# One pace for attention's background steps in all three token groups of a hybrid mLSTM, attention and expert block

## Chip, cores and metric

The kernel runs on one core of a Trainium2 chip. The metric is the device time of one execution in microseconds (us). An execution has five engines that matter here, each with its own queue of instructions in a fixed order: PE (TensorE, matmuls), DVE (VectorE), ACT (ScalarE), POOL (GpSimd, which here issues the gathers) and SP (SyncE, which issues the other DMAs).

## What is computed

One decoder block on x, 1024 tokens of 1024 values, in float32:

```python
h = rmsnorm(x, norm1_g) * (1 + sc1) + sh1
mq, mk, mv, mo, mi, mf, dq, dk, dv = split(h @ w_in)
hm = rmsnorm(mlstm_chunkwise(silu(conv(mq, mk)), mv, mi, mf)) * sigmoid(mo)
od = rmsnorm(softmax(dq1 @ dk1.T) @ dv - lam * softmax(dq2 @ dk2.T) @ dv) * c
x = x + g1 * (concat(hm, od) @ w_out)
h2 = rmsnorm(x, norm2_g) * (1 + sc2) + sh2
q = h2 @ w_query
...
x = x + g2 * sum over 8 heads and 16 experts of gate * gelu(h2 . u[e]) * v[e]
out = rmsnorm(x, final_g)
```

The attention is causal, has 4 heads, and each head has two score matrices of 64 values per key (the differential form). The expert stage picks, for each token and head, 16 of 16384 experts by two half keys.

## The kernel before

The 1024 tokens are 8 blocks of 128, in three groups of 2, 3 and 3 blocks (group 0, 1, 2). Each group goes through the same front stages, one after the other: `front_T` (normalize and transpose), `front_proj` (L692, all input projections), `front_mix` (L774, what is left of attention and mLSTM, then the norm of the mixed rows, `mix_end` L644), `front_out` (projection by w_out), `front_norm2` and `front_keys` (the query projection and the top 16 of each half). After the third group comes the dense part (L1338 scores, L1370 values), in which the experts of some token blocks are computed as full matmuls over the table. For the other blocks the rows of the chosen experts are gathered: POOL issues an indirect DMA for each (gu L1024, gv L1076, gvr L1057), DVE multiplies the row of u by the token (L1028), and PE or DVE sums the rows of v (`ga` L1090 on PE, L1064 on DVE).

**Background steps.** Work that is not the main line of a group is written as Python generators. Each is an entry [generator, rate, credit] in the list `background`. `tick()` (L306) adds the rate to the credit of every entry, and takes a step of it for each whole credit:

```python
w[2] += w[1]
while w[2] >= 1.0:
    w[2] -= 1.0
    more = next(w[0], False)
```

`tick()` is called once after each 256 KB weight tile of a projection (`proj_T` L390, `proj_R` L410), after each score matmul in `att_S` (L579), and on three of four steps of the loop in `front_mix`. Other entries are the gathers (rate 1.6), the gate tables (oh L1255, ps_g L1242, stg L1244; rate 1.5) and the mLSTM steps.

**Attention's steps.** `attention(o)` (L745) works on units, one for each head and block. With nb blocks in the group it has 4 heads times nb units and 2\*4\*nb + 1 steps, that is 17 in group 0 and 25 in groups 1 and 2:

```python
att_S(units[0])
yield
for k, u in enumerate(units):
    if k + 1 < len(units):
        att_S(units[k + 1])
    yield
    att_T(u)
    att_V(u)
    yield
```

`att_S` makes the scores on PE (ps_S L605, mask L608), their maximum on DVE (ast L609), the exponentials on ACT (ae L598) and the difference on DVE (ae L618). `att_T` transposes them (ps_at L629, aT L631), `att_V` multiplies by the values (ps_o L638). The first unit of a head also loads that head's keys and values (`att_load`, akT L572, avh L574) through SP. These two tiles share one tag of two buffers, so the next head's akT can be loaded when the last score matmul of this head is done, and its avh when the last L638 is done. A third user of that tag is the row g1r (L230) that `front_out` loads.

`front_proj` first projects dq, dk and dv, then puts the entry for attention into `background` (L707, L708), and then runs the projections of the mLSTM q, k, v and output gate. Between the two lie 32 weight tiles, so 32 ticks, in every group. The rate is AR[o.k], with AR = [0.6, 0.5, 0.3] (L63). By the ticks, all 17 steps are taken in group 0 (at tick 29), 16 of 25 in group 1, and 9 of 25 in group 2. The rest is run by the loop in `front_mix`:

```python
for _ in o.att[0]:
    k += 1
    if k % 2 or k % 4 == 0:
        next(steps, None)
        tick()
```

The tile framework then places the instructions: it orders each engine's instructions by its own model of times, with the program's order as a guide. The static order of each engine is therefore the program's only roughly.

Of the kernel before, what the change touches and what calls it, by code (L numbers as in the profile page):

```python
# [28 lines left out]
HD = 4  # L29
# [22 lines left out]
def kernel(ctx: ExitStack, tc: tile.TileContext, x, c_col, ada_w, ada_b, ada_bc, n1c,  # L52
# [7 lines left out]
    LPACE = ()  # L60
    PJ = 0
    ALT = 1
    AR = [0.6, 0.5, 0.3]  # L63
    SOG = [8, 0, 8]
    DEF = 0
    N1G = 2
# [491 lines left out]
    def att_heads(t0, nb, dq, mix):  # L558

        ms = fr.tile([P, 2, NBM, HD], F32, tag="ams", name="ams", bufs=1)  # L560
        units = []
        for h in range(HD):
            for b in range(nb):
                u = Unit()
                u.h, u.b, u.i, u.end = h, b, t0 + b, t0 + nb
                u.dq, u.mix, u.ms, u.first, u.units = dq, mix, ms, b == 0, units
                units.append(u)
        return units, ms
# [52 lines left out]
    def att_T(u):  # L621

        i, e = u.i, u.e
        u.aT = []
        for s0 in range(0, i + 1, 4):
            m = min(4, i + 1 - s0)
            pt = bank("ps_at")
            for j in range(m):
                nc.tensor.transpose(pt[:, j * P:(j + 1) * P], e[:, (s0 + j) * P:(s0 + j + 1) * P], ident)  # L629
            aT = fr.tile([P, 512], F32, tag="t2", name="aT", bufs=T2)  # L630
            nc.scalar.activation(aT[:, :m * P], pt[:, :m * P], AF.Copy)  # L631
            u.aT.append(aT)

    def att_V(u):
        h, b, i = u.h, u.b, u.i
        po = bank("ps_o")
        for s0 in range(i + 1):
            nc.tensor.matmul(po[:, :P], u.aT[s0 // 4][:, s0 % 4 * P:(s0 % 4 + 1) * P], u.vh[:, s0], start=s0 == 0, stop=s0 == i)  # L638
        mv = u.mix[b][:, 512 + h * P:512 + (h + 1) * P]
        nc.scalar.activation(mv, po[:, :P], AF.Copy, scale=u.r)  # L640
        junk = fr.tile([P, P], BF16, tag="ajunk", name="ajunk", bufs=1)
        nc.scalar.activation(junk, po[:, :P], AF.Square, scale=u.r, accum_out=u.ms[:, 1, b, h:h + 1])
# [49 lines left out]
    def front_proj(o):  # L692

        n, nb, t0 = o.n, o.nb, o.t0
# [9 lines left out]
        nc.sync.dma_start(vd_d[t0 * P:t0 * P + n, :].rearrange("(b p) e -> p b e", p=P), vst[:, :nb])  # L704
        o.a_, o.b_ = mlstm_rows(o.hT, nb)
        o.mix = [fr.tile([P, D], F32, tag="rows", name="mix", bufs=RB) for _ in range(nb)]
        o.att = [attention(o), AR[o.k], 0.0]  # L707
        background.append(o.att)  # L708
        overlapped.append(o)
        o.qk = []  # L710
# [34 lines left out]
    def attention(o):  # L745

        units, o.ams = att_heads(o.t0, o.nb, o.dq, o.mix)
# [9 lines that stand above are left out]
# [694 lines left out]
    front_T(gs[0])  # L1451
    for k, o in enumerate(gs):
        front_proj(o)
        front_mix(o)
        front_out(o)
# [109 lines left out]
```

## Time and profile before

| what | us |
|---|---|
| median of 3 runs (smallest to largest) | 2989.22 (2983.14 to 2993.66) |
| the profiled execution | 2983.2 |
| its span in the trace | 2981.3 |
| PE busy in the span | 2783.4 (93%) |
| DVE busy in the span | 2382.0 (80%) |
| ACT busy, POOL busy | 973.6 (33%), 1282.8 (43%) |
| DMA, mean | 302 GB/s |

The stages by time, from the lines that run in them: group 0 to about 209.5 us, group 1's front until its mix ends at 598.5 us, its output and keys and the projections of group 2 until about 1061 us, group 2's mix until 1184 us, group 2's keys until about 1413 us, the last gate tables and gathers until 1583 us, and the dense part until the end at 2981.3 us. Busy shares over the whole span average these stages; a stage is read from its own window.

### The profile page before, as it was taken

What the parts mean: (1) busy time and instruction counts of PE and PEld (TensorE: products, weight loads), DVE (VectorE), ACT (ScalarE), POOL (GpSimd) and SP (SyncE); (2) the same over time, 40 slices, a digit from 0 to 9 for tenths busy, and PEclk for the clock granted to TensorE, in tenths of its full rate; (3) what the DMA queues carried; (4) which work ended last, traced back from release to release, by engine and by line L of the source; (5) the groups of instructions that cost most, each with busy time, mean ns of one, the idle gap of its engine ahead of it and who ended that gap; (6) DMA issues with size and microseconds to landing.
All of it is one profiled execution on the core that took longest, in us unless ns stands there. A gap on an engine that the chain in (4) does not pass through costs nothing.

```text
span 2981.3 us, 40087 instructions
## 1 busy us (share of the span) xinstructions
PE 2783.4 (93%) x13686; PEld 2076.9 (70%) x13686; DVE 2382.0 (80%) x5489; ACT 973.6 (33%) x1695; POOL 1282.8 (43%) x1083
## 2 busy tenths in 40 slices
PE   6899999689999997999995999999999999999998
PEld 5547757465556765766574878878777788877786
DVE  5634999856997687357977988889988889988876
ACT  1432344312235445232453322322322323322232
POOL 0000266654555453334654555545554444544400
PEclk9989999689999999999997999999999999999999
DMA  8745699999998888998788999999899999999962
GB/s 280 252 138 180 209 360 336 324 350 339 325 345 306 305 299 293 350 332 293 280 309 284 337 335 334 332 340 340 313 339 322 331 341 324 338 323 317 318 230 70
DMA packets 396848, 900.00 MB, mean 302 GB/s; under 512 B 34770, under 2 KB 184274, under 8 KB 392548
## 3 DMA queue, kind: packets, MB, share of 16 engines
q0 software_dynamic: 147456, 536.94, 50.1%
q1 hardware_dynamic: 249188, 360.51, 35.9%
q8 instruction: 108, 1.77, 0.2%
q14 instruction: 96, 0.79, 0.1%
HBM read 846.97 MB, written 50.35 MB: 301 GB/s over the span
## 4 chain that ended last, share of the span: by engine, by line
PE 50%; DVE 18%; DMA 13%; issue 11%; POOL 5%; ACT 2%; SPq 0%; DVEq 0%; POOLq 0%; ACTq 0%
PE ps_pj L403 11%; PE ps_dS L1338 9%; PE ps_dA L1370 9%; DMA Gt<-G_d 8%; PE ps_pj L423 7%; DVE gu L1028 4%; PE ps_g L1242 3%; PE ga L1090 3%; POOL gvr L1057 3%; DVE ga L1064 2%; DMA gu<-in_peer_u_dram,ei 2%; PE ps_S L605 2%; DVE dvs L1364 1%; DMA gv<-in_peer_v_dram,eT 1%; PE ps_tr L379 1%
## 5 line engine op out<-in xcount | busy, mean ns | idle before, releaser
L1024 POOL DMA_INDIRECT gu<-in_peer_u_dram,ei x512 | 657.3, 1284 | 928.6 <-DVE sv L912 347.9
L1370 PE MATMUL ps_dA<-dvs,W 128*128 128x512 f32 x2976 | 720.8, 396 | 56.9 <-ACT W L1348 27.4
L1338 PE MATMUL ps_dS<-dhT,us 128*128 128x512 f32 x3072 | 731.0, 391 | 1.2 <-POOL us L1331 1.2
L1370 PEld LDWEIGHTS ps_dA<-dvs,W 128*128 128x128 f32 x2976 | 566.1, 191 | 188.9 <-ACT W L1348 27.4
L1028 DVE SCALAR_TENSOR_TENSOR gu<-gu,h2r 128x1024 f32<-128x1024 f32 x512 | 620.1, 1222 | 72.3 <-DMA gu<-in_peer_u_dram,ei 59.1
L1338 PEld LDWEIGHTS ps_dS<-dhT,us 128*128 128x128 f32 x3072 | 576.2, 188 | 129.4 <-issue 8.0
L1057 POOL DMA_INDIRECT gvr<-in_peer_v_dram,ei x256 | 301.5, 1178 | 339.0 <-DVE ga L1064 184.4
L1076 POOL DMA_INDIRECT gv<-in_peer_v_dram,eT x256 | 275.8, 1077 | 266.0 <-PE ga L1090 148.2
L1064 DVE SCALAR_TENSOR_TENSOR ga<-gvr,w,ga 128x1024 f32<-128x1024 f32 x254 | 326.9, 1287 | 1.7 <-issue 0.3
L1363 ACT ACTIVATE dvs<-dv 128x512 fp32r<-128x512 f32 x248 | 155.7, 628 | 368.4 <-PE ps_dA L1370 164.5
L403 PE MATMUL ps_pj<-hT,wr 128*128 128x384 f32 (+1 forms) x768 | 233.7, 459 | 3.1 <-ACT ae L598 2.9
L403 PE MATMUL ps_pj<-h2T,wr 128*128 128x384 f32 (+1 forms) x768 | 231.2, 454 | 0.0
L1339 ACT ACTIVATE ge<-ps_dS 128x512 f32<-128x512 f32 x128 | 76.5, 598 | 424.4 <-PE ps_dS L1338 413.3
L1244 ACT ACTIVATE stg<-ps_g 128x512 f32<-128x512 f32 x128 | 134.0, 1064 | 238.0 <-PE ps_g L1242 164.1
L403 PEld LDWEIGHTS ps_pj<-hT,wr 128*128 128x128 f32 x768 | 144.9, 193 | 79.5 <-issue 9.8
L1255 DVE TENSOR_TENSOR oh<-iotah,dT 128x1024 f16<-128x1024 f16 x128 | 102.2, 804 | 118.5 <-PE ps_g L1242 94.7
L403 PEld LDWEIGHTS ps_pj<-h2T,wr 128*128 128x128 f32 x768 | 142.2, 190 | 73.3 <-issue 9.9
L423 PE MATMUL ps_pj<-wr,hT 128*128 128x256 f32 (+1 forms) x672 | 182.1, 425 | 3.5 <-DMA wr<-in_w_in_dram 2.7
L1364 DVE TENSOR_TENSOR dvs<-dv,dvs 128x512 fp32r<-128x512 f32 x248 | 171.9, 698 | 16.4 <-ACT dvs L1363 16.4
L1347 DVE SCALAR_TENSOR_TENSOR ge<-ge,Gt 128x512 f32<-128x512 f32 x128 | 87.3, 692 | 119.1 <-DMA Gt<-G_d 112.9
L423 PEld LDWEIGHTS ps_pj<-wr,hT 128*128 128x128 f32 x672 | 128.5, 197 | 45.4 <-issue 23.8
L1377 DVE TENSOR_TENSOR dacc<-dacc,ps_dA 128x512 f32<-128x512 f32 x240 | 156.1, 683 | 4.6 <-PE ps_dA L1370 4.6
(294 smaller groups left out, 3333.1 us busy)
## 6 DMA issues: line engine op xcount, KB each, us to landing
u<-in_peer_uT_dram SPq DMA_DIRECT2D x128, 512.0 KB
dv<-in_peer_v_dram SPq DMA_DIRECT2D x248, 256.0 KB
wr<-in_w_in_dram SPq DMA_DIRECT2D x168, 256.0 KB
G_d<-stg SPq DMA_DIRECT2D x32, 1024.0 KB
Gt<-G_d SPq DMA_DIRECT2D x15, 2048.0 KB
wmod<-in_ada_w_dram SPq DMA_DIRECT2D x48, 512.0 KB
wr<-in_peer_w_query_dram SPq DMA_DIRECT2D x96, 256.0 KB
wr<-in_w_out_dram SPq DMA_DIRECT2D x48, 256.0 KB
```

Of the source, the lines that this page charges most:

```text
L403: nc.tensor.matmul(out[f], w2[:, kh, f * P:(f + 1) * P], hT[:, kb, :n], start=kb == 0 and f % k == 0, stop=kb == NC - 1 and f % k == k - 1)
L423: nc.tensor.matmul(out[f], hT[:, kb, f * P:(f + 1) * P], wk[:, kh], start=kb == 0 and f % k == 0, stop=kb == NC - 1 and (f % k == k - 1 or ...
L1024: nc.gpsimd.indirect_dma_start(out=u, out_offset=None, in_=pu, in_offset=bass.IndirectOffsetOnAxis(ap=o.ei[:, k:k + 1], axis=0))
L1028: nc.vector.scalar_tensor_tensor(u, u, 1.0, o.h2, op0=OP.mult, op1=OP.mult, accum_out=o.z[:, k:k + 1])
L1057: nc.gpsimd.indirect_dma_start(out=vt, out_offset=None, in_=pv, in_offset=bass.IndirectOffsetOnAxis(ap=o.ei[:, k:k + 1], axis=0))
L1064: nc.vector.scalar_tensor_tensor(o.acc, vt, o.w[:, k:k + 1], o.acc, op0=OP.mult, op1=OP.add)
L1076: got = nc.gpsimd.indirect_dma_start(out=vt, out_offset=None, in_=pv, in_offset=bass.IndirectOffsetOnAxis(ap=o.eT[:, t:t + 1], axis=0))
L1338: nc.tensor.matmul(ps, us[:, a, c], hT[:, b, c, sl], start=c == 0 and i == 0, stop=c == NC - 1 and i == 2)
L1363: nc.scalar.activation(vs[:, 0], v, AF.Copy)
L1364: nc.vector.tensor_sub(vs[:, 1], v, vs[:, 0])
L1370: nc.tensor.matmul(pacc[tb], w[:, a, tb * P:(tb + 1) * P], vs[:, b], start=jj == 0 and i == 0, stop=jj == J - 1 and i == 2)
L1377: nc.vector.tensor_add(o, o, pacc[tb])
```

## The change

The list AR is deleted, and the rate of the attention entry is the number of its steps divided by 32: 17/32 = 0.53 in group 0, 25/32 = 0.78 in groups 1 and 2. So in every group the last step of attention is taken with the last tick of the projections, and `front_mix` is left with no step of attention, only with the mLSTM outputs and `mix_end`. The 9 and 16 steps that its loop ran in groups 1 and 2 are gone from there, and with them the 7 and 12 ticks that it gave to the other background entries. No instruction is added or removed; the order changes.

```diff
--- before.py
+++ after.py
@@ -60,7 +60,6 @@
     LPACE = ()
     PJ = 0
     ALT = 1
-    AR = [0.6, 0.5, 0.3]
     SOG = [8, 0, 8]
     DEF = 0
     N1G = 2
@@ -704,7 +703,7 @@
         nc.sync.dma_start(vd_d[t0 * P:t0 * P + n, :].rearrange("(b p) e -> p b e", p=P), vst[:, :nb])
         o.a_, o.b_ = mlstm_rows(o.hT, nb)
         o.mix = [fr.tile([P, D], F32, tag="rows", name="mix", bufs=RB) for _ in range(nb)]
-        o.att = [attention(o), AR[o.k], 0.0]
+        o.att = [attention(o), (2 * HD * nb + 1) / 32.0, 0.0]
         background.append(o.att)
         overlapped.append(o)
         o.qk = []
```

Below, rows of each engine's order stand as they are issued; x16 means 16 in a row. The line numbers of the changed kernel are one lower, since L63 is gone (L605 is L604 there).

**PE, the end of group 1.** ps_S is a score matmul, ps_at a transpose of probabilities, ps_o their product with the values, ps_tr the transposes of the mixed rows with which `front_out` begins, ga a sum of gathered rows. Before, these rows end it:

```order
L605 MATMUL ps_S<-akT,dq 128x512
L605 MATMUL ps_S<-akT,dq 128x128
L608 LDWEIGHTS identb
L608 MATMUL ps_S<-mask_gt,identb 128x128
L629 MATMUL ps_at<-ident,ae 128x128 x4
L638 MATMUL ps_o<-avh,aT 128x128 x4
L629 MATMUL ps_at<-ident,ae 128x128 x5
L638 MATMUL ps_o<-avh,aT 128x128 x5
L1044 MATMUL ga<-ident,w 128x128
L1047 MATMUL ga<-ident,ef_3993 128x128
L377 MATMUL ps_tr<-ident,mix 128x128 x24
L423 MATMUL ps_pj<-wr,mT 128x256 x10
```

Before them, back to the last `L423 ... ps_pj<-wr,hT`, stand three more units without any projection. In the changed kernel:

```order
L422 MATMUL ps_pj<-wr,hT 128x256 x8
L604 MATMUL ps_S<-akT,dq 128x128
L607 LDWEIGHTS identb
L607 MATMUL ps_S<-mask_gt,identb 128x128
L628 MATMUL ps_at<-ident,ae 128x128 x4
L1043 MATMUL ga<-ident,w 128x128
L1046 MATMUL ga<-ident,ef_3992 128x128
L637 MATMUL ps_o<-avh,aT 128x128 x4
L628 MATMUL ps_at<-ident,ae 128x128 x5
L637 MATMUL ps_o<-avh,aT 128x128 x5
L1089 MATMUL ga<-gv,strip_182 32x256 x16
L376 MATMUL ps_tr<-ident,mix 128x128 x24
```

Now the last eight matmuls of the projections stand inside the last score unit, and two units of transposes and products follow instead of five; 16 ga stand ahead of the transposes.

**PE, the switch from one head to the next in group 1.** From the last score unit (128x512 and 128x128) of a head to the first (128x384) of the next, before:

```order
L605 MATMUL ps_S<-akT,dq 128x512
L605 MATMUL ps_S<-akT,dq 128x128
L608 LDWEIGHTS identb
L608 MATMUL ps_S<-mask_gt,identb 128x128
L403 MATMUL ps_pj<-hT,wr 128x384 x16
L629 MATMUL ps_at<-ident,ae 128x128 x4
L638 MATMUL ps_o<-avh,aT 128x128 x4
L605 MATMUL ps_S<-akT,dq 128x384
L608 LDWEIGHTS identb
L608 MATMUL ps_S<-mask_gt,identb 128x128
```

and in the changed kernel:

```order
L604 MATMUL ps_S<-akT,dq 128x512
L402 MATMUL ps_pj<-hT,wr 128x384 x8
L604 MATMUL ps_S<-akT,dq 128x128
L607 LDWEIGHTS identb
L607 MATMUL ps_S<-mask_gt,identb 128x128
L628 MATMUL ps_at<-ident,ae 128x128 x4
L637 MATMUL ps_o<-avh,aT 128x128 x4
L604 MATMUL ps_S<-akT,dq 128x384
L607 LDWEIGHTS identb
L607 MATMUL ps_S<-mask_gt,identb 128x128
```

The 16 matmuls of a projection that stood between the last scores of a head and the first of the next are gone from there; this form is there twice in the changed kernel (both within the projections) and once before (in the tail).

**SP, the loads in group 1.** wr are the weight tiles, before:

```order
L574 DMA avh<-vd_d 128x5x128
L385 DMA wr<-in_w_in_dram 128x2x256 x6
L572 DMA akT<-kd_d 128x640
L385 DMA wr<-in_w_in_dram 128x2x256 x8
L574 DMA avh<-vd_d 128x5x128
L385 DMA wr<-in_w_in_dram 128x2x256 x4
L572 DMA akT<-kd_d 128x640
L385 DMA wr<-in_w_in_dram 128x2x256 x5
L385 DMA wr<-in_w_out_dram 128x2x256 x3
L574 DMA avh<-vd_d 128x5x128
```

and in the changed kernel:

```order
L573 DMA avh<-vd_d 128x5x128
L384 DMA wr<-in_w_in_dram 128x2x256 x6
L571 DMA akT<-kd_d 128x640
L384 DMA wr<-in_w_in_dram 128x2x256 x4
L573 DMA avh<-vd_d 128x5x128
L384 DMA wr<-in_w_in_dram 128x2x256 x4
L571 DMA akT<-kd_d 128x640
L384 DMA wr<-in_w_in_dram 128x2x256 x2
L573 DMA avh<-vd_d 128x5x128
L384 DMA wr<-in_w_in_dram 128x2x256 x6
L571 DMA akT<-kd_d 128x640
L384 DMA wr<-in_w_in_dram 128x2x256
```

All four loads of akT now stand among the weight tiles of w_in; the last one stood behind those of w_out before.

Two counts from the same orders: of the 512 products L1028 on DVE, 128 stand ahead of group 1's first L652 (`mix_end`) before and 134 in the change, and 256 ahead of group 2's in both; of the 1024 sums L1090 on PE (program instructions), 832 stand ahead of the dense part's first L1338 before and 800 in the change, and 1024 and 1000 ahead of its first L1370.

## Rows read from the trace of the kernel before

**Rows 1.** The page: busy time, share of the span and instructions of each engine.
```profile
PE 2783.4 (93%) x13686; PEld 2076.9 (70%) x13686; DVE 2382.0 (80%) x5489; ACT 973.6 (33%) x1695; POOL 1282.8 (43%) x1083
```

**Rows 2.** Windows: stretch us, length, busy of PE PEld DVE ACT POOL, PEclk, DMA, GB/s.
```profile
343.00:387.00 44.00, 44.00 (x169) 30.48 (x168) 41.33 (x116) 7.52 (x13) 28.58 (x25) 1.00 1.01 379
387.00:480.00 93.00, 88.50 (x319) 55.87 (x318) 90.39 (x221) 45.96 (x94) 66.12 (x46) 0.93 0.96 343
480.00:540.00 60.00, 57.19 (x308) 45.13 (x307) 50.71 (x114) 23.48 (x67) 39.58 (x34) 1.00 0.97 347
540.00:598.50 58.50, 28.15 (x83) 16.68 (x83) 51.10 (x134) 18.12 (x51) 37.19 (x30) 0.54 0.92 316
...
880.00:1061.00 181.00, 180.56 (x1085) 123.95 (x1078) 134.67 (x311) 86.14 (x166) 93.14 (x75) 0.97 0.89 308
1061.00:1159.00 98.00, 84.55 (x579) 53.13 (x577) 80.62 (x194) 48.57 (x108) 53.44 (x47) 0.95 0.89 321
1159.00:1184.00 25.00, 15.93 (x128) 12.54 (x129) 18.10 (x47) 15.24 (x30) 1.47 (x2) 0.85 0.78 268
...
1490.00:1583.00 93.00, 90.64 (x629) 69.07 (x621) 74.07 (x107) 48.48 (x53) 45.48 (x33) 1.00 0.83 296
1583.00:1610.70 27.70, 0.35 (x3) 0.26 (x3) 16.00 (x27) 2.70 (x5) 14.36 (x12) 0.50 0.94 341
1610.70:2981.00 1370.30, 1331.79 (x5760) 1089.67 (x5760) 1207.26 (x1665) 411.96 (x630) 614.37 (x494) 0.98 0.88 309
```

**Rows 3.** Waits of PE, 209.5 to 598.5 us: total us, times, longest.
```profile
PE ps_at L629 <- DVE ae L618: 16.0, 2, 10.7
PE ps_S L605 <- DMA akT<-kd_d: 7.8, 1, 7.8
PE ps_tr L377 <- DVE mix L652: 4.5, 1, 4.5
```

**Rows 4.** Timeline of PE, end of group 1: start, us, line, count, [idle before].
```profile
539.10 0.61 PE L629 MATMUL ps_at<-ident,ae 128*128 128x128 f32 x4
540.39 1.16 PE L638 MATMUL ps_o<-avh,aT 128*128 128x128 f32 x8 [0.69 <-ACT aT L631]
549.35 1.61 PE L605 MATMUL ps_S<-akT,dq 64*128 64x384 f32 x2 [7.81 <-DMA akT<-kd_d]
...
589.59 1.30 PE L629 MATMUL ps_at<-ident,ae 128*128 128x128 f32 x5 [10.71 <-DVE ae L618]
...
598.55 1.28 PE L377 MATMUL ps_tr<-ident,mix 128*128 128x128 f32 x4 [1.24 <-DVE mix L652]
```

**Rows 5.** Timeline of SP's queue: three of the loads of akT (L572).
```profile
416.48 0.34 SPq L572 DMA_DIRECT2D akT<-kd_d  x1
...
539.12 0.34 SPq L572 DMA_DIRECT2D akT<-kd_d  x1
...
1118.75 0.32 SPq L572 DMA_DIRECT2D akT<-kd_d  x1
```

**Rows 6.** Timeline of PE: the scores that need rows 5's first and third load.
```profile
434.09 0.91 PE L605 MATMUL ps_S<-akT,dq 64*128 64x384 f32 x2
...
1126.45 1.55 PE L605 MATMUL ps_S<-akT,dq 64*128 64x512 f32 x4
```

**Rows 7.** The page's costliest groups: the product of a gathered row, on DVE.
```profile
L1028 DVE SCALAR_TENSOR_TENSOR gu<-gu,h2r 128x1024 f32<-128x1024 f32 x512 | 620.1, 1222 | 72.3 <-DMA gu<-in_peer_u_dram,ei 59.1
```

**Rows 8.** Waits of PE, 1061 to 1184 us, then 1413 to 1700 us.
```profile
PE ps_g L1242 <- ACT stg L1244: 12.1, 10, 3.3
...
PE ps_dA L1370 <- ACT W L1348: 27.4, 1, 27.4
```

**Rows 9.** Timeline of SP's queue at the start of the dense part.
```profile
1582.18 0.33 SPq L1247 DMA_DIRECT2D G_d<-stg  x1
...
1591.69 22.90 SPq L1285 DMA_DIRECT2D Gt<-G_d  x2
```

**Rows 10.** Timeline of PE: the last sums of rows of v.
```profile
1558.32 1.06 PE L1090 MATMUL ga<-gv,strip 128*32 128x256 f32 x14
```

## Prediction, made before the changed kernel was run

> **What bounds the kernel now.** Read in this order: the page's busy shares, then the windows by stage, then PE's waits, then the timeline around the waits. PE is busy 93% of the span [rows 1], so only what PE does not do can be won. The windows [rows 2] say where that is. The dense part is PE's own: 1331.8 of 1370.3 us, and nothing in it is touched. From 880 to 1061 us PE is busy 180.6 of 181. Three places are left that the change reaches. Group 1's mix, 540 to 598.5 us, has PE busy 28.2 of 58.5 us, and the granted clock there is 0.54, about the lower of PE's two levels (1.2 against 2.4 GHz). Group 2's mix, 1061 to 1184 us, has PE idle for 98.0 - 84.6 + 25.0 - 15.9 = 22.5 us. The start of the dense part has a bubble of 27.4 us [rows 2, 8].
>
> In those idle 30 us of group 1's mix PE waits for akT once (7.8 us) and for DVE's ae twice (16.0 us) [rows 3]. The timeline shows the five units that are left there: scores, transposes and products follow one another with nothing between them [rows 4]. The reader is to see next that this is not PE's stage alone: over 343 to 598.5 us DVE is busy 41.3 + 90.4 + 50.7 + 51.1 = 233.5 of 255.5 us (91%), and the DMA engines 0.92 to 1.01 of the time [rows 2]. The ae that PE waits for is late because products of gathered rows, 1.22 us plus about 0.09 us for the accumulator, stand ahead of it on DVE [rows 7]. So group 1 is held by two queues at once, DVE and DMA, and PE's idle time collects at its end.
>
> **The change part by part.** No instruction is added or removed. All scores, transposes and products go from the mixes into the projections.
>
> *Group 0.* The rate falls from 0.6 to 0.53; attention ends three ticks later and its last unit meets the mix. PE waits there for `mix_end` already, 4.5 us [rows 3]. A little of the last unit's chain joins it: I take +3, with -3 (the wait shrinks) and +8 (one wait of PE for ae at the mean of the two in rows 3, 8.0 us) as ends.
>
> *Group 1.* The five units in the tail are gone but for two steps of transposes and products. PE's idle 30 us would go if PE were the bound. It is not: ahead of the first `mix_end` instruction DVE has the same work as before and 6 more products (134 against 128), 6 x 1.31 = 7.9 us. DVE needs 233.5 + 7.9 = 241.4 us in any case. With no idle time at all on DVE the mix comes at 255.5 - 241.4 = 14 us earlier; with the same idle share, 241.4 / 0.914 = 264, it comes 8.6 us later. DMA says the same: six more rows of 512 KB are 3.1 MB, at 343 GB/s 9 us of a queue that is 0.95 taken. Between -14 and +9 I take -3, near the middle, since the waits of a tail without cover shrink but both queues stay full.
>
> The new waits lie inside this. Two switches of head now have no projection between the last scores and the next head's first ones. akT can be issued only when the last score matmul is done, because of the two buffers; in the one place where the old order did that, it was issued at 539.12, the scores began at 549.35, 10.2 us later, and PE stood for 7.8 us, with the transposes and products as its only cover (2.4 us) [rows 4, 5]. With projections between, the same load was hidden: issued at 416.48, its scores ran at 434.09 [rows 5, 6]. The third switch has mLSTM matmuls between; between nothing and 7.8 us I take 4. Sum of PE's waits: 7.8 + 7.8 + 4 - 7.8 = +12 us. PE has room for them, since it waits for DVE in this group anyway, and so they are not added to the -3; the case where they are is a rival. Queued behind the waiting score matmul is the next projection's work, and behind that the wr buffers and SP's loads.
>
> The Trainium skill, "DMA: Bandwidth & Descriptors", section "Anatomy of one DMA — SWDGE (gpsimd) path", gives a fit of a fixed 2.0 us plus the bytes over 436e3 per us; for akT (128 x 640 x 4 B = 328 KB) an estimate by it is 2.75 us, and by that the three switches would cost under 2 us together. That page's path is not SP's, and in the row 10.2 us passed from issue to scores beside gathers and weights, so the row decides.
>
> *Group 2.* Here 16 of 25 steps leave the mix, and the work ahead of `mix_end` on DVE is unchanged in count (256 products in both). DVE is busy 80.6 of 98 us from 1061 to 1159 [rows 2], less full than in group 1, so PE's idle time can go: 98.0 - 84.6 = 13.4 us, and some 4 us of PE work at the lower clock (granted clock 0.95 and 0.85 [rows 2]; an estimate). Of this some comes back: the projections need DVE and ACT for their evacuation, and ACT already holds PE's ps_g up for 12.1 us here [rows 8]; I give back 4. The three switches of head have covers of 7 us and more in the new order: the shortest holds transposes, products, four times eight ps_g and eight ga, much as the one in rows 5 and 6 that went without a wait (issued at 1118.75, scores at 1126.45). I give 2 for them. So -17 + 4 + 2 = -11, with ends of -18 (nothing comes back) and +5 (the ps_g waits come back in full and the ticks that the mix gave to the tables are missed).
>
> *Start of the dense part.* The mixes give 19 ticks less to the gathers, 19 x 1.6 = 30 steps. At the dense part's first score 800 sums of v rows are done instead of 832, and at its first value matmul 24 are left; 40 stand between the last ps_g and that matmul, each gather feeding four, so 10 gathers of v with as many of u between. POOL issued 33 in the 93 us ahead of 1583 [rows 2], so 20 take about 56 us, against 52 us from the last sums at 1558.3 [rows 10] to the first value matmul at 1610.7 [rows 2]. That is about a tie with the bubble, which has its own cause: the read of Gt issued at 1591.69 takes its time behind the last G_d write at 1582.18 [rows 9]. In the new order no u, dv or output transfer stands between those two, which is some us in favour. I take +3, ends -6 (that gain) and +20 (the gathers are late by a further 15 to 20 us).
>
> *Sum.* 3 - 3 - 11 + 3 = -8 us. Against the profiled execution, 2983.2, that is 2975; that execution is 6 us under the median of the runs, 2989.2, so against the median it is **2981**.
>
> **The rivals.**
>
> *PE's tail in group 1 really goes.* If DVE's 91% is slack that merely spreads out, the mix loses PE's idle 30.4 us, and its 28.2 us of work at clock 0.54 would take 15.2 at full clock, 13 less. Back come the end of the chain, from the last transposes at 589.6 to the mix at 598.6 [rows 4], 9 us, and the six products, 8: -26 in group 1, and with the other terms (+3 - 11 + 3) -31, about 2958. For it speak PE's waits [rows 3]; against it the DVE and DMA columns [rows 2]. The Trainium skill, "TensorE: Matmul & The Clock Gate", section "Part 1: The HAM clock gate (the "warmup" mystery)", has an idle TensorE fall back to the low clock; the window at 0.54 agrees, and its 13 us are what that rule would give back here.
>
> *Nothing reaches the end.* What the mixes save is waited for again at the dense start or in the queues of gathers: 2986 to 2992. DMA at 0.88 or more in every one of these windows but one [rows 2] speaks for it.
>
> *Slower: the switches of head hold up the projections.* The mechanism is the two buffers of akT and avh. In the changed order akT waits for the last score with no projection behind it, in PE's fixed order. It decides if the load takes longer than its cover (10.2 against 2.4 us [rows 4, 5]) and DVE, starved by the standing projections, cannot use the time. Then group 1 is +8.6 (DVE at its old share) and +12 (the waits), group 0 and the dense start are +6 together, group 2 gives -11: +16, about 3005. For it speaks that the only such place in the trace did stall in full; against it that PE has 30 us to give in this group.
>
> That the change doesn't do what it says is excluded by the order: in groups 1 and 2 the steps have left the mixes.
>
> **How the numbers follow.** A measurement of this kernel can tell about 0.3%, 9 us, from no change, so the bounds are 2980 and 2998. The main case has 0.50 and a range of its own of 2969 to 2992; the forecast lies almost on the bound, so half of it counts as faster and half as the same. PE's tail has 0.13 (faster), nothing 0.10 (same), slower 0.27. That gives faster 0.25 + 0.13 = 0.38, same 0.25 + 0.10 = 0.35, slower 0.27. Leaving out the far half of either outer case, the range is 2962 to 3008.
>
> **What would show it.** Right: between the last projection of group 1 and its `mix_end` PE is idle for under 10 us instead of 30, while the window from 343 us to `mix_end` is within 14 us of the old length with DVE at 93% or more; PE waits for akT three times in the projections, 4 to 8 us each; group 2's mix is some 11 us shorter; the bubble at the dense start is 25 to 35 us. Wrong: the stretch to group 1's `mix_end` is shorter by over 20 us (DVE was no bound), or longer by over 10 with akT waits of that size (the slower rival); or a first value matmul that waits for ga.

## The result and the profile after

The changed kernel took 3040.38 us (median of 6, 3034.06 to 3046.61) against 2990.91 for the kernel before in the same runs: a ratio of 1.0168, 95% interval 1.0147 to 1.0188. It is slower by about 50 us, outside the predicted range (2962 to 3008) and on its slow side. The profiled execution has a span of 3036.9 us against 2981.3, 55.6 more; some 6 us of that are the two executions themselves, since the one of the kernel before lies 7.7 us under its median and this one 1.7. From the timelines of PE:

| us from the start | before | after | difference |
|---|---|---|---|
| group 0, first transpose of mixed rows | 209.5 | 208.1 | -1.4 |
| group 1, the same | 598.6 | 625.5 | +26.9 |
| group 1, last key scores | 783.5 | 802.7 | +19.2 |
| group 2, first transpose of mixed rows | 1181.6 | 1221.2 | +39.6 |
| group 2, last key scores | 1410.8 | 1448.2 | +37.4 |
| first value matmul of the dense part | 1610.7 | 1647.3 | +36.6 |
| end of the span | 2981.3 | 3036.9 | +55.6 |

So the loss comes in three places: group 1 up to its mix (28 us), group 2 from the end of group 1's keys to its own mix (20), and the dense part itself (19); the keys of group 1 give 8 back. The page's busy line of the changed kernel:

```profile
PE 2802.3 (92%) x13686; PEld 2082.3 (69%) x13686; DVE 2388.1 (79%) x5489; ACT 975.8 (32%) x1699; POOL 1274.6 (42%) x1083
```

PE's busy time rose by 19 us at the same count of instructions [rows 1]; the four more on ACT are ACT_TABLE_LOAD (65 for 61 in the traces). The windows cut at stages show where. The columns are those of [rows 2]; the stretches are group 1 from its first scores to its last projection, from there to its mix, group 2 from first scores to its mix, its last keys to the first value matmul, and the dense part. The kernel before:

```profile
392.65:535.72 143.07, 136.06 (x591) 95.70 (x591) 132.17 (x317) 63.30 (x149) 99.61 (x74) 0.95 0.96 341
535.72:598.55 62.83, 32.13 (x103) 19.02 (x102) 54.71 (x141) 19.64 (x56) 38.53 (x32) 0.57 0.93 322
893.91:1181.57 287.66, 264.99 (x1709) 180.29 (x1708) 217.10 (x509) 141.62 (x291) 138.74 (x116) 0.96 0.87 306
...
1410.80:1610.70 199.90, 164.23 (x1117) 117.50 (x1113) 167.59 (x423) 89.01 (x95) 109.99 (x80) 0.91 0.84 298
1610.70:2981.30 1370.60, 1331.79 (x5760) 1089.67 (x5760) 1207.26 (x1665) 411.96 (x630) 614.37 (x494) 0.98 0.88 309
```

and the changed kernel:

```profile
391.24:600.86 209.62, 168.23 (x661) 112.58 (x660) 180.60 (x416) 71.74 (x184) 151.11 (x105) 0.84 0.92 324
600.86:625.49 24.63, 8.97 (x64) 6.06 (x65) 18.91 (x69) 9.15 (x22) 12.37 (x11) 0.65 0.68 235
915.90:1221.19 305.29, 278.93 (x1730) 184.50 (x1729) 223.56 (x517) 146.74 (x296) 137.96 (x124) 0.92 0.86 300
...
1448.16:1647.29 199.13, 170.46 (x1157) 120.46 (x1155) 173.44 (x432) 90.31 (x96) 127.54 (x91) 0.89 0.89 314
1647.29:3036.90 1389.61, 1333.44 (x5810) 1088.30 (x5810) 1201.72 (x1662) 412.19 (x632) 604.74 (x492) 0.99 0.87 306
```

Group 1 (first two rows of each): 205.9 us became 234.3. The tail shrank from 62.8 to 24.6, as the order promised, but the projections grew from 143.1 to 209.6, and the granted clock there fell from 0.95 to 0.84. DVE's busy share, which was 91% over the two stretches (186.9 of 205.9), is 85% (199.5 of 234.3): DVE stands more than before. Group 2 (third row) grew by 17.6 us, of which 13.9 are busy time of PE. Much of that is work that has moved into this stretch: it holds 16 more matmuls of a projection (112 for 96) and 16 more ga, and 8 ps_g fewer. A stretch with about the same work in both kernels runs from the end of group 1's keys to group 2's mix, before and after:

```profile
783.50:1181.57 398.07, 372.54 (x2276) 247.74 (x2272) 322.12 (x898) 177.65 (x340) 199.89 (x167) 0.96 0.90 315
```

```profile
802.70:1221.19 418.49, 384.14 (x2264) 251.60 (x2263) 325.04 (x909) 182.12 (x343) 184.90 (x166) 0.93 0.86 298
```

It is 20.4 us longer: 11.6 of PE's busy time, with 12 matmuls fewer and a granted clock of 0.93 instead of 0.96, and 8.8 us of idle time. The start of group 2's scores shows where, before (one row) and after (two rows, the second up to 22 us ahead of the mix):

```profile
893.91:1000.00 106.09, 105.94 (x602) 68.49 (x601) 78.78 (x179) 50.69 (x90) 55.84 (x44) 0.98 0.88 300
```

```profile
915.90:1025.00 109.10, 96.36 (x540) 56.03 (x540) 84.08 (x187) 50.74 (x95) 55.70 (x48) 0.86 0.87 302
1025.00:1199.00 174.00, 169.25 (x1086) 117.86 (x1085) 124.81 (x279) 80.41 (x175) 76.52 (x71) 0.98 0.85 300
```

PE was idle for 0.2 us there and is now idle for 12.7, with the granted clock at 0.86 instead of 0.98; its waits in these 109 us are for ACT first of all:

```profile
PE ps_g L1241 <- ACT stg L1243: 6.1, 4, 2.8
PE ps_S L604 <- ACT ae L597: 3.1, 1, 3.1
PE ps_pj L402 <- ACT ae L597: 1.3, 1, 1.3
```

The stretch ahead of the dense part did not change (199.9 and 199.1).

PE's longest waits in group 1 after the change, 343 to 626 us, where [rows 3] stood before:

```profile
PE ps_o L637 <- DMA avh<-vd_d: 12.6, 2, 10.9
PE ga L1089 <- DMA gv<-in_peer_v_dram,eT: 10.5, 1, 10.5
PE ps_S L604 <- DMA akT<-kd_d: 10.4, 2, 8.3
...
PE ps_at L628 <- DVE ae L617: 4.3, 2, 2.9
```

The two waits for DVE's ae (16.0 us) have fallen to 4.3 us, and waits for transfers have risen from 7.8 to 33.5 us. The timeline of PE at the two waits for akT, at the longer one for avh and at the mix:

```profile
432.29 1.61 PE L604 MATMUL ps_S<-akT,dq 64*128 64x384 f32 x2 [2.03 <-DMA akT<-kd_d]
...
453.53 0.50 PE L628 MATMUL ps_at<-ident,ae 128*128 128x128 f32 x3
464.90 1.62 PE L637 MATMUL ps_o<-avh,aT 128*128 128x128 f32 x6 [10.88 <-DMA avh<-vd_d]
...
482.35 1.16 PE L637 MATMUL ps_o<-avh,aT 128*128 128x128 f32 x8 [0.69 <-ACT aT L630]
491.86 1.61 PE L604 MATMUL ps_S<-akT,dq 64*128 64x384 f32 x2 [8.35 <-DMA akT<-kd_d]
...
623.63 1.93 PE L1089 MATMUL ga<-gv,strip 128*32 128x256 f32 x16 [10.48 <-DMA gv<-in_peer_v_dram,eT]
625.49 4.77 PE L376 MATMUL ps_tr<-ident,mix 128*128 128x128 f32 x24
```

and SP's queue for the three loads:

```profile
426.45 0.34 SPq L571 DMA_DIRECT2D akT<-kd_d  x1
...
451.29 0.37 SPq L573 DMA_DIRECT2D avh<-vd_d  x1
...
481.14 0.56 SPq L571 DMA_DIRECT2D akT<-kd_d  x1
```

At 481.14 akT is issued and its scores begin at 491.86, 10.7 us later: what [rows 4, 5] showed at the end of group 1 now happens among the projections. At 451.29 avh is issued and the first product that needs it runs at 464.90, 13.6 us later. The akT of the first switch took less, 5.8 us from 426.45 to 432.29. The 16 ga that the order puts ahead of the mixed rows' transposes stand behind a wait of 10.5 us for their gather. For most of that time the mixed rows were not there either, since DVE writes the first of them only at 621.62 (598.15 before):

```profile
621.62 1.14 DVE L651 SCALAR_TENSOR_TENSOR mix<-hm,ams,mo 128x128 f32<-128x128 f32 x4
```

At the mix this wait is worth some 3.5 us (an estimate: from the end of the first of these four, 621.97, to 625.49). The waits of DVE in group 1 for gathered rows of u, before and after:

```profile
DVE gu L1028 <- DMA gu<-in_peer_u_dram,ei: 7.3, 8, 2.8
```

```profile
DVE gu L1027 <- DMA gu<-in_peer_u_dram,ei: 19.9, 28, 4.1
```

### The profile page after: what moved, and what is told of

Same layout as the page of the kernel before. It is cut to its first block, busy times and chain, and to the rows that moved or that the text cites. A ratio compares the mean times of both kernels' runs of the same rounds, so it can differ in the third digit from the quotient of the medians.

```text
span 3036.9 us, 40065 instructions
## 1 busy us (share of the span) xinstructions
PE 2802.3 (92%) x13686; PEld 2082.3 (69%) x13686; DVE 2388.1 (79%) x5489; ACT 975.8 (32%) x1699; POOL 1274.6 (42%) x1083
## 4 chain that ended last, share of the span: by engine, by line
PE 50%; DVE 17%; DMA 16%; issue 10%; POOL 3%; ACT 3%; SPq 0%; DVEq 0%; POOLq 0%; ACTq 0%
PE ps_dA L1369 12%; PE ps_dS L1337 10%; PE ps_pj L402 10%; DMA Gt<-G_d 7%; PE ps_pj L422 6%; DVE gu L1027 4%; DMA gu<-in_peer_u_dram,ei 3%; PE ps_g L1241 3%; DVE ga L1063 3%; PE ga L1089 3%; POOL gu L1023 2%; PE ps_S L604 2%; DMA wmod<-in_ada_w_dram 1%; DVE dvs L1363 1%; DVE dacc L1376 1%
## 5 line engine op out<-in xcount | busy, mean ns | idle before, releaser
L1369 PE MATMUL ps_dA<-dvs,W 128*128 128x512 f32 x2976 | 718.8, 395 | 47.1 <-DVE dvs L1363 30.7
L402 PE MATMUL ps_pj<-hT,wr 128*128 128x384 f32 (+1 forms) x768 | 242.1, 471 | 1.9 <-ACT ae L597 1.3
L1243 ACT ACTIVATE stg<-ps_g 128x512 f32<-128x512 f32 x128 | 133.5, 1061 | 235.0 <-PE ps_g L1241 181.2
L1338 ACT ACTIVATE ge<-ps_dS 128x512 f32<-128x512 f32 x128 | 76.3, 596 | 397.2 <-PE ps_dS L1337 394.9
L1089 PE MATMUL ga<-gv,strip 128*32 128x256 f32 x2048 | 158.0, 411 | 33.0 <-DMA gv<-in_peer_v_dram,eT 32.6
L1254 DVE TENSOR_TENSOR oh<-iotah,dT 128x1024 f16<-128x1024 f16 x128 | 95.8, 755 | 109.2 <-PE ps_g L1241 98.0
L1363 DVE TENSOR_TENSOR dvs<-dv,dvs 128x512 fp32r<-128x512 f32 x248 | 168.2, 682 | 12.9 <-ACT dvs L1362 12.7
```

The costliest lines, as they stand in the source:

```text
L402: nc.tensor.matmul(out[f], w2[:, kh, f * P:(f + 1) * P], hT[:, kb, :n], start=kb == 0 and f % k == 0, stop=kb == NC - 1 and f % k == k - 1)
L1089: mm = nc.tensor.matmul(o.acc[c * 32:(c + 1) * 32, q * QW:(q + 1) * QW], st[:, q, 31 + 32 * i - r:63 + 32 * i - r], vt[:, c * QW:(c + 1) * ...
L1363: nc.vector.tensor_sub(vs[:, 1], v, vs[:, 0])
L1369: nc.tensor.matmul(pacc[tb], w[:, a, tb * P:(tb + 1) * P], vs[:, b], start=jj == 0 and i == 0, stop=jj == J - 1 and i == 2)
```

## The experiments

Every run was compared with the kernel before on the same chip. "Mix 1" and "mix 2" are the first transposes of mixed rows in groups 1 and 2 in the run's trace (598.6 and 1181.6 us before, 625.5 and 1221.2 in the changed kernel); "group 2's stretch" is from its first scores to mix 2 (287.7 and 305.3).

**One group at a time.** The list AR kept, one number changed in each of three kernels:

```diff
-    AR = [0.6, 0.5, 0.3]
+    AR = [17 / 32, 0.5, 0.3]
...
+    AR = [0.6, 25 / 32, 0.3]
...
+    AR = [0.6, 0.5, 25 / 32]
```

> Only group 0 gets the new rate (0.53 for 0.6). Theory A (group 1's projections stand because the next head's akT and avh wait for the two shared buffers, with PE at half clock after it): within 6 us of before, since group 0's heads have few keys and its mix came 1.4 us earlier in the changed kernel. Theory B (the ticks that front_mix no longer gives delay the gathers, and the dense part pays): within 6 us, since group 0 gave no ticks. If it is slower by over 10 us, the order of everything behind it is sensitive to any edit, and neither theory can be read from single groups.

Measured: 2989.56 us, ratio 1.0006 (0.9982 to 1.0031). Group 0 costs nothing, and the program does not answer to every edit.

> Only group 1 gets the new rate (0.78 for 0.5). Theory A: group 1's mix comes 20 to 30 us later, as in the changed kernel (598.5 to 625.5), with akT and avh waits of PE of 15 to 25 us in sum, and 15 to 30 us of it reach the end. Theory B: 7 lost ticks are 11 gather steps; the end is 5 to 10 us later, and most of it shows only at the dense start.

Measured: 3031.07, ratio 1.0133 (1.0103 to 1.0164). Mix 1 at 624.3, waits for akT of 11.2 us and for avh of 11.2. Group 1 alone costs 42 us, more than theory A asked for; mix 2 is already 33 us late.

> Only group 2 gets the new rate (0.78 for 0.3). Theory A: group 2's switches of head are covered, so the end is between 10 us earlier and 10 us later. Theory B: 12 lost ticks are 19 gather steps of about 2 to 3 us each on POOL; the sums of rows of v end 30 us or more later and stand between the value matmuls, the end is 20 to 30 us later.

Measured: 3023.00, ratio 1.0108 (1.0075 to 1.0140). Mix 1 at 602.3, mix 2 at 1205.0: group 2's stretch is 310.8 us, 23 longer. Group 2 alone costs 34. The last sums are late (1617 us, before 1558), as theory B asked, but still ahead of the first value matmul (1642), and 23 of the 43 us by which the profiled execution is longer stand ahead of mix 2, where neither theory had a loss. The three add up to 77, so they overlap in the 50 of the whole change.

One of the three switches of head in group 2 of that run shows how a "cover" can fail. PE from the last products of a head to the first scores of the next:

```profile
951.07 1.99 PE L638 MATMUL ps_o<-avh,aT 128*128 128x128 f32 x14
956.98 1.10 PE L1242 MATMUL ps_g<-oh 128*128 128x128 f16 x8 [3.92 <-ACT stg L1244]
959.22 1.10 PE L1242 MATMUL ps_g<-oh 128*128 128x128 f16 x8 [1.14 <-ACT stg L1244]
960.25 2.07 PE L605 MATMUL ps_S<-akT,dq 64*128 64x512 f32 x2
```

and the load of akT in SP's queue:

```profile
947.25 0.52 SPq L572 DMA_DIRECT2D akT<-kd_d  x1
```

13 us pass from the load's issue to the scores. No wait for akT is in the list, since the last thing PE waited for was ps_g: the two batches of ps_g that stand there as cover wait for ACT themselves (3.9 and 1.1 us). Why the order has them there is not shown. At the other two switches of that run PE is idle for 0.5 and 0.8 us.

In the changed kernel itself the covers hold. At its first switch in group 2, PE and then SP's queue:

```profile
971.14 1.74 PE L637 MATMUL ps_o<-avh,aT 128*128 128x128 f32 x14
974.01 1.10 PE L1241 MATMUL ps_g<-oh 128*128 128x128 f16 x8 [1.12 <-DVE ast L613]
975.04 1.55 PE L604 MATMUL ps_S<-akT,dq 64*128 64x512 f32 x4
```

```profile
967.38 0.34 SPq L571 DMA_DIRECT2D akT<-kd_d  x1
```

From the load's issue to the scores pass 7.7 us here and 9.7 and 14.6 at the other two switches, and PE waits 1.1 us in all three together.

**The lost ticks.** The changed kernel, with the ticks given back:

```diff
+        for _ in range([0, 7, 12][o.k]):
+            next(steps, None)
+            tick()
         for _ in steps:
             pass
         mix_end(
```

> The changed kernel with the 7 and 12 ticks given back in front_mix of groups 1 and 2, beside the mLSTM outputs. Theory A: at least 25 of the 50 us remain (group 1's mix still at 620 us or later). Theory B: 3000 us or less, with the last sums of rows of v ahead of the dense part's first value matmul again.

Measured: 3043.92, ratio 1.0182 (1.0135 to 1.0230), with mix 1 at 619.8. The last sums are early again (1564 us, against 1677 in the changed kernel) and the dense part is 16 us shorter (1373.6), but mix 2 is 12 us later (1232.9) and the gate tables end 16 us later. Theory B falls: the work that the ticks carry is paid for wherever it stands.

**Three buffers instead of two** for akT and avh. There is no room for it unless t2 gives up two buffers, so there are two controls:

```diff
-    WB, T2, C8, KV, ... = 7, 8, 4, 2, ...
+    WB, T2, C8, KV, ... = 7, 6, 4, 2, ...
...
+    WB, T2, C8, KV, ... = 7, 6, 4, 3, ...
```

> The changed kernel with 6 instead of 8 buffers of the tag t2, to make room; the control of the next run. All theories: within 15 us of the changed kernel (3040), with akT and avh waits of PE of 15 to 25 us in group 1.

Measured: 3043.29, ratio 1.0163 (1.0145 to 1.0181); mix 1 at 624.6, mix 2 at 1225.9.

> The same with three buffers instead of two for akT and avh. Theory A (the handover of the two buffers holds the projections in group 1): PE's waits for akT and avh in group 1 fall under 6 us, group 1's mix comes 12 to 25 us earlier than in its control, and at least half of that reaches the end. Rival D (akT and avh are late because DMA is full and SP issues them behind weight tiles, or PE would only wait for DVE instead): the waits stay or others take their place, and the end stays within 6 us of the control.

Measured: 3007.46, ratio 1.0048 (1.0031 to 1.0065): 36 us faster than its control. Mix 1 at 602.3, mix 2 at 1181.4. PE's waits for these loads in group 1, in the control:

```profile
PE ps_S L604 <- DMA akT<-kd_d: 11.3, 3, 8.1
PE ps_o L637 <- DMA avh<-vd_d: 11.1, 1, 11.1
```

and with three buffers (with the longest wait that is left):

```profile
PE ps_tr L376 <- DVE mix L651: 13.4, 1, 13.4
...
PE ps_o L637 <- DMA avh<-vd_d: 1.4, 1, 1.4
```

The akT of head 1 is issued at 397.7 us instead of 430.7, ahead of its need by a head. Theory A holds for group 1: 22 us at mix 1, of which 11 are left at the end of its keys (794.6 us against 805.5). DVE is busy 180.6 us from group 1's first scores to mix 1, in the control 198.0, so part of its work has moved behind the mix. The same edit gives 26 us in group 2's stretch (283.1 against 309.5), where the list of waits has none for akT or avh.

> The kernel before with 6 instead of 8 buffers of t2: within 15 us of before.

Measured: 2994.35, ratio 1.0010 (0.9999 to 1.0020).

> The kernel before with 6 buffers of t2 and three for akT and avh. Theory A: the one wait of 7.8 us in group 1's tail goes; PE waits for DVE there anyway, so the end is 0 to 8 us earlier than its control. Rival D: no change.

Measured: 2983.86, ratio 0.9967 (0.9947 to 0.9987). With the old rates the third buffer is worth about 10 us against its control, and this version is faster than both kernels. So the third buffer has to be read from all four: the new rates cost 49 us with two buffers (3043.29 against 2994.35) and 24 with three (3007.46 against 2983.86). About half of the loss goes with the third buffer, and half stays.

**The handover taken away in another way:** in the group with the end given, all heads use one load, with two buffers as before (the attention of heads 1 to 3 is left out in that sense). This also takes six transfers per group off the DMA queues.

```diff
-        if u.first:
+        if u.first and (u.h == 0 or u.end != 5):
             att_load(u)
...
-            if w.h == u.h:
+            if w.h == u.h or u.end == 5:
                 w.kT, w.vh = kT, vh
```

> The changed kernel, but in group 1 all four heads use the keys and values of head 0, loaded once (the attention of heads 1 to 3 of that group is left out in that sense); buffers as in the changed kernel. Theory A (the handover of the two buffers): group 1's mix comes at about 600 us instead of 625, and the end 10 to 25 us earlier than the changed kernel (3015 to 3030). Rival E (the third buffer helped in another way, by another order of the whole program): group 1's mix stays after 615 us.

Measured: 3033.09, ratio 1.0153 (1.0124 to 1.0182). Mix 1 at 609.2 (16 us earlier), mix 2 at 1201.7 (20 earlier), first value matmul at 1632.3 (15 earlier); but the dense part took 1401.5 us, 12 longer, so that by the two ratios 4 us of it reach the end.

> The same in group 2 alone. Theory A extended to group 2 (what stands at its switches of head as cover is itself waiting, so the handover costs there too, without a wait for akT in the list): from the keys of group 1 to group 2's mix 387 to 400 us instead of 418, and the end 10 to 25 us earlier than the changed kernel. Rival F (group 2 is slower because the scores in the projections share five PSUM banks with them): that stretch stays within 8 us of 418.

Measured: 3018.62, ratio 1.0111 (1.0083 to 1.0138). Group 2's stretch is 298.0 us, from group 1's keys to mix 2 it is 409.9 instead of 418.5; by the two ratios the end is 17 us earlier. The stretch is longer than theory A asked for (387 to 400) and just outside rival F's 8 us.

> The kernel before with the new rate in group 2 alone, and group 2's heads all on the keys and values of head 0, loaded once (that leaves out the attention of its heads 1 to 3 in that sense). Without the single load this rate cost 34 us (3023), and group 2 took 311 us from its first scores to its mix. Theory A in group 2: 285 to 296 us for that stretch and an end at 2990 to 3008. Rival F (PSUM banks, or the order itself): 303 us or more, and an end at 3013 or later.

Measured: 3024.22, ratio 1.0121 (1.0092 to 1.0150), as without the single load (3023). Group 2's stretch is 300.6 us, 10 of its 23 us back, which is neither theory's; the end has nothing of it, as rival F asked.

> The changed kernel with one load of keys and values in group 1 and in group 2 (heads 1 to 3 of both left out in that sense). Theory A: about as with three buffers, 3000 to 3015, group 2's mix at 1180 to 1195. If only a part of the third buffer's gain was the handover: 3016 to 3030.

Measured: 3031.56, ratio 1.0150 (1.0115 to 1.0185). Mix 1 at 605.5, mix 2 at 1201.8; the end is later than either expectation. So the handover, taken away by itself, is worth 16 to 20 us up to the mixes, and by the ratios 4, 17 and 5 us at the end (group 1, group 2, both); the 36 us of the third buffer are more than that. What else it does (the akT of group 2's second head is issued at 894.8 us instead of 969.2, so its units are placed elsewhere) stays open.

**Three buffers, with the ticks or for group 2 alone.**

> The changed kernel with three buffers for akT and avh (6 of t2) and the 7 and 12 ticks given back to the mixes. Theory B in its smaller form (the lost ticks are what is left, about 15 us, after the handover is gone): the last sums of rows of v end before the first value matmul again and the end is at 2985 to 3000. Rival G (what the ticks move is paid elsewhere, as in the changed kernel with two buffers): within 6 us of the version with three buffers and no ticks, 3007.

Measured: 3035.47, ratio 1.0149 (1.0111 to 1.0187): 28 us slower than three buffers without the ticks (30 by the two ratios), and outside both expectations. Mix 2 is 12 us later, the gate tables end at 1633 us instead of 1599. Giving the ticks back costs here.

> A try at a faster kernel: three buffers (6 of t2), the new rate in group 2 alone. By the three-buffer runs group 2's stretch to its mix is 387 against 404 us, and the gathers give some of it back: 2970 to 2985, faster than the kernel before. If the gathers give back all of it: 2985 to 2998.

Measured: 2994.02, ratio 1.0022 (1.0004 to 1.0040). Group 2's stretch is 289.9 us against 293.9 with the old rate and three buffers, but the stretch from group 2's keys to the first value matmul is some 13 us longer and the dense part takes 1384.6 us against 1374.4. What group 2 gains is more than given back: by the ratios this is 16 us slower than three buffers with the old rates.

**Late sums in the dense part.** Of the last 128 gathers of v for PE's sums, 32 are left out:

```diff
+        psums.append(o)
+        o.lim = P if len(psums) < 2 else P - 32
...
-                if summing and nv < P:
+                if summing and nv < summing[0].lim:
```

> The changed kernel with the last 32 of the 128 gathers of v of the last block that PE sums left out. Theory H (the dense part is 19 us longer because sums of v rows are left over into it): the last sums end before the first value matmul, the dense part falls from 1389.6 to under 1377 us. Rival I (the dense part is longer for another reason, such as fewer products of u rows done): it stays over 1384.

Measured: 3072.61, ratio 1.0273 (1.0243 to 1.0302). The last sums end at 1506 us, and the dense part still takes 1389.2, as rival I asked. PE's waits in the dense part, of the kernel before, the changed kernel and this one:

```profile
PE ps_dA L1370 <- DVE dvs L1364: 19.0, 13, 3.1
...
PE ps_dA L1370 <- DVE dacc L1377: 2.7, 7, 0.9
```

```profile
PE ps_dA L1369 <- DVE dvs L1363: 30.7, 13, 9.6
PE ps_dA L1369 <- DVE dacc L1376: 7.7, 13, 3.5
```

```profile
PE ps_dA L1374 <- DVE dvs L1368: 25.3, 8, 5.5
PE ps_dA L1374 <- DVE dacc L1381: 11.9, 12, 4.7
```

With two smaller entries for dacc (1.6 us in the changed kernel, 4.9 in this one) PE waits for DVE's results (dvs, dacc) 21.7, 40.0 and 42.1 us. That is nearly all of the 19 us; why DVE is later there is not shown.

> The kernel before with the same 32 gathers left out; the control of the run ahead of this one. The gathers are not on its path at the dense start, so the end is 0 to 20 us earlier than before and the dense part stays at 1365 to 1375. The difference between these two kernels is, by theory H, 28 to 38 us instead of 50.

Measured: 3038.50, ratio 1.0161 (1.0110 to 1.0212): less work, and 52 us slower, where 0 to 20 us faster was expected. Up to 1413 us it is the kernel before; then PE waits for the one-hot tables that DVE makes, at the end of the gate tables:

```profile
PE ps_g L1247 <- DVE oh L1261: 50.6, 19, 8.3
```

The kernel before waited there for no oh that the list shows. With fewer sums ahead of it the same stretch got another order, with products of rows in front of the tables on DVE (the cause is argued; the wait is shown). The dense part of this control takes 1383.1 us, not the 1365 to 1375 expected, and the two kernels differ by 34 us, which lies in the range that theory H asked for (28 to 38). With the order ahead changed in both, the pair decides little. Other runs do: one group's rate alone (e2_g1) and group 2 with one load (j_g2_oneload) have no sum left over in the dense part, and it takes 1384.4 and 1386.8 us there. So the sums are not needed for a long dense part.

**Half-way rates.** AR = [0.6, 0.64, 0.3], then [0.6, 0.5, 0.54]:

> The kernel before with 0.64 in group 1, half way between 0.5 and 0.78 (the latter alone cost 42 us). Theory A: a switch of head costs once it comes inside the projections without cover; one or two of the three do here, so the end is at 3000 to 3020 and group 1's mix at 605 to 620 us. Rival K (any other order of this program costs 30 us or more, as the runs with fewer gathers did, by chance): 3020 or later, or within 5 us of before.

Measured: 3001.51, ratio 1.0046 (1.0024 to 1.0069); mix 1 at 610.2 us. Its two largest waits in group 1:

```profile
PE ps_at L629 <- DVE ae L618: 12.5, 1, 12.5
PE ps_o L638 <- DMA avh<-vd_d: 10.1, 2, 5.1
```

> The kernel before with 0.54 in group 2, half way between 0.3 and 0.78 (the latter alone cost 34 us). If the cost grows with the steps that stand in the projections: 3000 to 3015, with group 2's first scores to its mix at 293 to 305 us. Rival K (chance of the order): outside of that.

Measured: 2998.58, ratio 1.0034 (1.0012 to 1.0055). Group 2's stretch is 310.0 us, as long as at 0.78 (310.8), but less of it reaches the end. For group 1 the cost at the end goes 0, 12, 42 us with the rate, and both of its numbers lie where theory A put them. For group 2 the end goes 0, 9, 34, but both numbers lie outside what was expected, and the stretch does not grow between the two higher rates: that its cost is one of the order and not of the rate (rival K) is not excluded.

## Why the prediction was wrong

*Group 0 (+3).* Right within its bounds: -1.4 us, and 2989.56 us when it stands alone.

*Group 1 (-3, between -14 and +9).* It was +28.4. The step that failed is "PE has room for them, since it waits for DVE in this group anyway, and so they are not added". The akT waits were named, but they came to 10.4 us in two places (8.35 and 2.03) where 7.8 + 7.8 + 4 had been the estimate, and DVE did not use the time. Both its columns moved against the bounds: it was busy 199.5 us, not 186.9 + 7.9, and it idled 34.7 us instead of 19.0, with 19.9 us of waits for gathered rows instead of 7.3. The upper end, "with the same idle share", had no ground: DVE wrote the first mixed row 23.5 us later. That a standing PE holds up the scores and projections that DVE and the gathers wait for is the reading of these rows, and argued; that the handover is at the root of the lateness at the mix is shown by the runs without it (22 us earlier with three buffers, 16 with one load). Two waits were not in the list at all: avh (12.6 us), whose handover has the same cause (its wait falls from 11.1 to 1.4 us with a third buffer), and the gather ahead of the transposes (10.5 us, some 3.5 of them at the mix). The prediction's own sign for the slower rival, over 10 us longer with waits for akT, is what came. The idle time also brought the lower clock into the projections (0.84), the loss that the tail alone had had before.

*Group 2 (-11).* It was +17.6 from first scores to mix. The step that failed is "so PE's idle time can go: 98.0 - 84.6 = 13.4 us", with only 4 us given back. The idle time did go from there (4.8 of 174 us from 1025 to 1199), but it came back in the projections ahead of it, 12.7 us in 109 where there had been 0.2, in waits for ACT's ae and stg, and the granted clock fell there with it. So about the whole 13.4 came back instead of 4, and no clock was won. The cover of the three switches, "covers of 7 us and more" with 2 us for them, held: 1.1 us of waits. With three buffers the stretch is 283.1 us with the new rates, against 293.9 with the old ones and 284.3 with the old ones and two buffers; with one load it is 298.0 and 300.6. So even the sign of the term without the handover is not settled, and why a third buffer helps here, where no switch waits long, stays open.

*Start of the dense part (+3).* Right in size: keys to first value matmul changed by -0.8 us. Behind the last ps_g 32 of the sums stand in the trace (64 matmuls, two to a sum), where the prediction counted 40; PE waits 16.5 us for their gathers, in place of the bubble of 27.4.

*The dense part ("nothing in it is touched").* Wrong by 19 us. But for 24 sums left over into it its matmuls are the same, and PE waits 18.3 us longer in it for DVE. The sums are not needed for that; what the cause is stays open.

*The rivals.* The slower one had the right mechanism and place in group 1, and a chance of 0.27. Its price (3005) was low because it kept -11 for group 2 and had nothing for the dense part, and gave DVE its old share. The rival in which PE's tail goes was half right: the tail went (PE idle 15.7 us there instead of 30.7), and the projections paid for it. For the rival in which nothing reaches the end, the reading "but one" of the DMA column is off by one: two windows of [rows 2] lie under 0.88, at 0.78 and 0.83. The fit of the Trainium skill, "DMA: Bandwidth & Descriptors", section "Anatomy of one DMA — SWDGE (gpsimd) path", would have made the switches nearly free (2.75 us for a load, an estimate by it; its path is not SP's). The loads that PE waited for took 5.8, 10.7 and 13.6 us from issue to use, so the trace was right to decide.

What the runs leave of the 50 us: about 25 go with a third buffer, beyond the 10 that it gives the kernel before as well. Of the handover by itself 16 to 20 us show at the mixes, and only 4 to 17 at the end. What else the third buffer does is not explained, and neither are the 24 us that stay with it: at the end of group 2's keys that run is 8 us ahead of the old rates with three buffers (1409.3 us against 1417.1 in the profiled executions), and it loses 25 in the stretch ahead of the dense part and 10 in it.

## What to carry to other kernels

Before work with loads of its own is moved in among the matmuls of a full engine, look at the one place where the old order already did that and price every handover of its buffers by it, keys and values both; a wait that cost little in a tail stops everything behind it when it stands in the main line. Count as cover only work whose own inputs are ready. Idle time that work leaves behind in one stage can come back in the stage that takes the work up, so price that stage too. And where two buffers are handed over at each step, a third may be worth more than a better place: here it made the kernel before about 10 us faster. Its worth has to be measured on both kernels, or what it gives to either is put down to the change.

## What was not expected of the hardware and the order

A load of 328 KB that was issued when its consumer was next took 5.8, 10.2, 10.7 and 13.6 us to its use, with the DMA engines 92% busy in these stretches. Leaving work out can cost: 32 gathers less made the kernel before 52 us slower and the changed one about 31. The order of the instructions that are left changed with it; that this is the cause is argued.
